# Mixing layer of a decoder block: T1 and T3 made in place as one tile, T4 and T2 made chunk by chunk in four idle tiles

## The chip, the cores and the metric

The kernel runs on one core of one Trainium2 chip. The metric is the device time of one execution in microseconds (us), as the median of the runs of a kernel; the profile and the trace are those of one further execution.

## What is computed

The reference is one layer of a decoder trunk over 1024 tokens of width 1024 in float32. The part around the change is the end of the token mixers and the start of the gated MLP:

```python
merged = sigmoid(g_da) * (y_da @ w_br_da) + sigmoid(g_sw) * (y_sw @ w_br_sw)
x  = x + merged @ w_mix_out
xn = rmsnorm(x, norm_ffn_w)
u  = xn @ w_up                          # 1024 -> 2 * 2816
c  = causal depthwise convolution of u, width 3, plus conv_b
x  = x + (silu(gate) * val) @ w_down    # gate, val: the halves of c
```

Before this stand the input projection and the two attentions, behind it a last rmsnorm. Every float32 matmul is done in three passes: both operands are split into a rounded high part and the rest (h and l), and the products h·h, h·l and l·h are added up. A split costs a cast on ScalarE and a subtraction on VectorE.

## The kernel before

Data lie transposed: 128 channels on the partitions, tokens along the free dimension, so x is eight chunks of 128 x 1024. The products with `w_up` are done with a seven-product scheme (Winograd's variant of Strassen) over 2 x 2 blocks. Chunk k (0 to 3) of the activations together with chunk k + 4 gives four blocks of 128 x 512: B11 and B12 are the token halves of chunk k, B21 and B22 those of chunk k + 4. From these come T1 = B12 - B11, T3 = B22 - B12, T2 = B22 - T1 and T4 = T2 - B21. The seven products are P1 = A11·B11, P2 = A12·B21, P5 = S1·T1, P7 = S3·T3, P3 = S4·B22, P6 = S2·T2 and P4 = A22·T4, where the A are blocks of a pair of weight tiles and the S are sums of them.

**The mixing layer, `mix` (L706 to L745).** Eight turns i, in the order of chunks 0, 4, 1, 5, 2, 6, 3, 7. Each has 48 matmuls with a tile of `w_mix` (L135 to L137, into `sc`), then VectorE adds x (L728), ScalarE stores x and scales it by the norm weight into a tile `xw` (L731), and ScalarE squares x (L740) while GpSimd adds the squares into `rstd` (L741). After every odd turn, `operands` (L747) makes the blocks of one k: it splits B11, B21, T1, T3 and B22 (each a cast L701 and a subtraction L702 of 128 x 512), with T1 and T3 first made on VectorE in small tiles (L758, L761), and T2 made unsplit on GpSimd (L764) into two tiles of the pool `cpl`, which the MLP later uses for its convolution. At i = 6 `sum_pair` (L78) makes the S of the first pair of weights on GpSimd (L87 to L90, into tiles `sf`).

**The up-projection, `hidden` (L777).** 22 turns j, one per pair of weight tiles. In turn 0 the first five products are done for k = 0 to 2; then the T2 are split (L800); then GpSimd rebuilds each B21 as the sum of its parts (L804), VectorE subtracts it from T2 to make T4 (L805), and T4 is split (L806); then the five products get k = 3, the squares are summed over the partitions by 16 small matmuls (L143), GpSimd makes the reciprocal root (L152), P6 and P4 follow, and eight transposes (L158) spread the root over the partitions, from where VectorE copies it (L818). In each later turn the order is P1, P2, P5, P6, P7, P3, P4, 84 matmuls (L773 to L775). `recombine` (L341) takes the seven sums from PSUM with one copy on ScalarE (L349) and seven operations on VectorE (L350 to L356); GpSimd scales the two results (L865); ScalarE begins the convolution (L868), VectorE adds its two other taps (L869, L870), ScalarE applies silu (L833) and VectorE multiplies (L834).

**The weights of a turn.** `sum_pair` loads g into a tile `raw` (L81) and v into a tile `rv` (L83) and makes two tiles of sums, `sa` (L87, L88: the S1 and S2) and `sb` (L89, L90: the S3 and S4), both from the pool `sfp`, which has two buffers, so each `sb` goes where the last `sb` was. `split_pair` (L92) casts (L100) and subtracts (L102): `wl<-raw` for A11 and A12, `sl<-sf` for the S, `wl<-rv` for A22. The sums of a turn are made some two turns ahead.

**What sets the order.** No order is written out by hand here. A planner walks the program with a cost for each instruction and gives each engine a fixed queue: an engine takes the first instruction in program order that is ready by these costs, and `high_priority` (L788) puts some ahead. On the chip each queue is worked off in that order. A tile of a pool can be written when the tile that had its buffer (or its place, where one pool was closed and another opened) has been read for the last time.

Of the kernel before, what the change touches and what calls it, by code (L numbers as in the profile page):

```python
# [47 lines left out]
class Trunk:  # L48
# [656 lines left out]
    def mix(self, mh, ml, mctx):  # L705


        nc, tc = self.nc, self.tc
        self.fctx = ExitStack()
        self.cpl = self.fctx.enter_context(tc.tile_pool(name="cpl", bufs=2, reuse_waits="tile"))  # L710
        self.xctx2 = ExitStack()
        xc = self.xctx2.enter_context(tc.tile_pool(name="xc", bufs=1, reuse_waits="tile"))
        self.B = {}
        xt = {(n, k, p): xc.tile([P, H2], F32R, name=f"{n}_{k}{p}") for n in ("B11", "B21", "T1", "T3", "B22") for k in range(4) for p in "hl"}
        self.sfp = self.xctx2.enter_context(tc.tile_pool(name="sfp", bufs=2, reuse_waits="tile"))
        self.t2 = [self.tl(self.cpl, [P, 2, H2], "c") for _ in range(2)]
        acc = self.rstd
        mact = lambda kc, hf: (mh[kc][:, hf * H2:(hf + 1) * H2], ml[kc][:, hf * H2:(hf + 1) * H2])
        with tc.tile_pool(name="xtp", bufs=2, side="right", reuse_waits="tile") as xtp:
            xw = {}  # L720
            for i, m in enumerate(self.mix_order):
                x2 = self.tl(xtp, [P, T], "x2")
                nc.sync.dma_start(x2, self.xT[m])
                w = self.next_w()
                ps = self.tl(self.psS, [P, T], "sc")
                self.mm3_both(ps, w, mact, late=(KC - 1,) if i == 0 else ())
                self.flush(0)
                nc.vector.tensor_tensor(x2, x2, ps, ALU.add)  # L728
                self.store(self.x2d[m], x2)
                xw[m] = self.tl(xtp, [P, T], "xw")  # L730
                nc.scalar.mul(xw[m], x2, self.vecs[:, C_NF + m:C_NF + m + 1])  # L731
                if i == 0:
                    nc.scalar.activation(acc, x2, AF.Square)
                if i == 6:
                    pair = self.sum_pair(self.wsrc.pop(0)[0], True)
                if i % 2:
                    self.operands(xt, xtp, xw, i // 2)
                for hf in range(2 if i else 0):
                    sq = self.tl(xtp, [P, H2], "t", bufs=3)
                    nc.scalar.activation(sq, x2[:, hf * H2:(hf + 1) * H2], AF.Square)  # L740
                    nc.gpsimd.tensor_tensor(acc[:, hf * H2:(hf + 1) * H2], acc[:, hf * H2:(hf + 1) * H2], sq, ALU.add)  # L741
            self.flush(0)
        mctx.close()
        self.pctx.close()
        return pair  # L745

    def operands(self, xt, xtp, xw, k):  # L747

        tt = self.nc.vector.tensor_tensor
        b11, b12, b21, b22 = (xw[kc][:, hf * H2:(hf + 1) * H2] for kc in (k, k + 4) for hf in range(2))  # L750

        def put(name, t):
            self.B[name, k] = self.split(xt[name, k, "h"], xt[name, k, "l"], t)
# [7 lines left out]
        tt(t3, b22, b12, ALU.subtract)  # L761
        put("T3", t3)
        put("B22", b22)
        self.nc.gpsimd.tensor_tensor(self.t2[k // 2][:, k % 2], b22, t1, ALU.subtract)  # L764
# [12 lines left out]
    def hidden(self, pair):  # L777
        nc, tc = self.nc, self.tc
        with ExitStack() as ctx:
            e = ctx.enter_context  # L780
            psF = e(tc.tile_pool(name="psF", bufs=8, space=PSUM, reuse_waits="tile"))
            self.psT = psF
            xc2 = e(tc.tile_pool(name="xc2", bufs=1, side="right", reuse_waits="tile"))
            self.uw = e(tc.tile_pool(name="uw", bufs=3, side="right", reuse_waits="tile"))
            tp = e(tc.tile_pool(name="tp", bufs=2, side="right", reuse_waits="tile"))
            prods = (("P1", "A11", "B11"), ("P2", "A12", "B21"), ("P5", "S1", "T1"), ("P7", "S3", "T3"),
                     ("P3", "S4", "B22"), ("P6", "S2", "T2"), ("P4", "A22", "T4"))
            with tc.high_priority(400):  # L788
                w0 = self.split_pair(*pair)
            for j in range(NF):  # L790
                w = self.next_w() if j else w0
                ps = {}
                if j == 0:

                    for name, a, b in prods[:5]:
                        ps[name] = self.tl(psF, [P, H2], "t")
                        self.product(ps[name], w[a], b, range(3), last=False)
                    for k in range(4):
                        t2 = self.t2[k // 2][:, k % 2]
                        self.B["T2", k] = self.split(*(xc2.tile([P, H2], F32R, name=f"T2_{k}{p}") for p in "hl"), t2)  # L800
                    for k in range(4):
                        t2 = self.t2[k // 2][:, k % 2]
                        b21 = self.tl(tp, [P, H2], ("s1", "u2", "u3", "u4")[k], bufs=1)
                        nc.gpsimd.tensor_tensor(b21, *(t.bitcast(F32) for t in self.B["B21", k]), ALU.add)  # L804
                        nc.vector.tensor_tensor(t2, t2, b21, ALU.subtract)  # L805
                        self.B["T4", k] = self.split(*(xc2.tile([P, H2], F32R, name=f"T4_{k}{p}") for p in "hl"), t2)  # L806
# [27 lines left out]
                nc.vector.tensor_tensor(c[0], c[0], c[1], ALU.mult)  # L834
# [214 lines left out]
```

## Time and profile before

| | |
|---|---|
| median of 3 runs | 1409.01 us (1406.46 to 1409.37) |
| profiled execution | 1411.19 us |
| span of its instructions | 1409.4 us |
| busy: PE, VectorE (DVE), ScalarE (ACT), GpSimd (POOL) | 97%, 69%, 44%, 33% |
| mean granted TensorE clock | 0.986 |
| mixing layer, first matmul to last | 616.5 to 704.8 us |
| up-projection, first matmul to last | 704.67 to 1144.3 us |

PE is the matmul engine, PEld its weight loads. A row of the timeline has the start and the length in us, the engine, the line, the operation, its output and inputs with the names of the program (numbers left out: B_0h can be B11, B21 or B22 of k = 0, and T_0h one of T1 to T4), a count, and in brackets the idle time of the engine ahead of it with what ended it. Rows with a count above 1 are several instructions merged, with their total time. A matmul row lasts 0.39 us because matmuls overlap; what one costs is the distance between two starts.

### The profile page before, as it was taken

How to read it: one execution, taken by the hardware profiler on the slowest of the kernel's cores; microseconds unless marked ns; L12 is line 12 of the kernel's file. 1: busy time of each engine (PE TensorE's matmuls, PEld its weight loads, DVE VectorE, ACT ScalarE, POOL GpSimd, SP SyncE). 2: the span in 40 equal slices, each digit the busy share in tenths (PEclk: the TensorE clock that was granted, in tenths of full speed). 3: DMA queues.
4: the chain of work that ended last, by engine and by line, in shares of the span. 5: the costliest groups of instructions: out<-in, count | busy, mean ns of one | idle time of the engine just before them, and what ended most of it. 6: DMA issues, size and time to landing. Idle time of an engine off the chain costs nothing.

```text
span 1409.4 us, 17228 instructions
## 1 busy us (share of the span) xinstructions
PE 1367.7 (97%) x6374; PEld 1121.9 (80%) x6374; DVE 972.8 (69%) x1408; ACT 624.6 (44%) x975; POOL 461.8 (33%) x326
## 2 busy tenths in 40 slices
PE   8899999999999999999999999999999999999997
PEld 6688888888888777878867778888888867888887
DVE  8966763887778855455499888888889896344332
ACT  8422322877756753334344333443333354233221
POOL 0446530000000033633476565555555441000001
PEclk9999999999999999999989999999999999999998
DMA  6244438755243263334411222222222258433432
GB/s 245 84 156 149 165 135 260 200 159 138 89 121 123 79 221 141 133 107 136 145 64 61 90 75 90 90 75 76 75 89 90 74 170 279 143 116 119 158 95 73
DMA packets 62196, 179.23 MB, mean 127 GB/s; under 512 B 6816, under 2 KB 13088, under 8 KB 62112
## 3 DMA queue, kind: packets, MB, share of 16 engines
q1 hardware_dynamic: 49648, 158.88, 35.2%
q10 hardware_dynamic: 12464, 19.25, 3.8%
q8 instruction: 50, 0.82, 0.2%
q14 instruction: 34, 0.28, 0.1%
HBM read 130.39 MB, written 47.71 MB: 126 GB/s over the span
## 4 chain that ended last, share of the span: by engine, by line
PE 56%; DVE 18%; issue 8%; POOL 7%; ACT 6%; DMA 4%; DVEq 0%; ACTq 0%; SPq 0%; POOLq 0%
PE d L900 16%; PE t L773 4%; PE t L774 4%; PE t L775 4%; POOL us L865 4%; PE g L135 3%; PE g L137 3%; PE g L136 3%; DVE wl L102 3%; PE sc L519 3%; DVE c L834 3%; DMA gr<-gd 2%; PE sc L137 2%; PE sc L135 2%; PE sc L136 2%
## 5 line engine op out<-in xcount | busy, mean ns | idle before, releaser
L900 PE MATMUL d<-h,wh 128*128 128x512 f32 (+1 forms) x680 | 202.7, 383 | 5.1 <-ACT h L701 2.3
L116 DVE TENSOR_TENSOR wl<-raw,wh 128x1024 fp32r<-128x1024 f32 (+1 forms) x79 | 98.6, 1248 | 144.3 <-ACT wh L114 140.0
L114 ACT CAST wh<-raw 128x1024 fp32r<-128x1024 f32 (+1 forms) x81 | 81.5, 1007 | 196.7 <-PE d L900 142.4
L900 PEld LDWEIGHTS d<-h,wh 128*128 128x128 f32 x680 | 126.2, 190 | 33.7 <-DVE h L702 5.2
L868 ACT ACTIVATE c<-us,vecs 128x1024 f32<-128x1024 f32 x44 | 54.8, 1248 | 168.6 <-POOL us L865 164.1
L900 PE MATMUL d<-h,wl 128*128 128x512 f32 (+1 forms) x340 | 123.9, 381 | 0.0
L100 ACT CAST sh<-sf 128x1024 fp32r<-128x1024 f32 x60 | 62.7, 1049 | 96.5 <-POOL sf L88 57.5
L865 POOL TENSOR_TENSOR us<-us,rstd 128x1024 f32<-128x1024 f32 x42 | 100.4, 2409 | 14.5 <-DVE us L355 10.2
L87 POOL TENSOR_TENSOR sf<-rv 128x512 f32<-128x512 f32 x29 | 40.4, 1393 | 191.7 <-DMA rv<-in_w_up 60.2
L869 DVE SCALAR_TENSOR_TENSOR c<-us,vecs,c 128x1024 f32<-128x1024 f32 x44 | 66.5, 1512 | 50.6 <-ACT c L868 50.6
L152 POOL TENSOR_TENSOR rs<-ms,mhalf 128x8 f32<-128x8 f32 (+2 forms) x9 | 13.7, 1518 | 245.0 <-DVE ms L150 236.3
L102 DVE TENSOR_TENSOR sl<-sf,sh 128x1024 fp32r<-128x1024 f32 x60 | 84.0, 1402 | 9.0 <-ACT sh L100 9.0
L137 PE MATMUL g<-xh,wl 128*128 128x512 f32 x224 | 89.4, 399 | 0.0
L136 PE MATMUL g<-xl,wh 128*128 128x512 f32 x224 | 89.2, 398 | 0.0
L135 PE MATMUL g<-xh,wh 128*128 128x512 f32 x224 | 88.9, 397 | 0.0
L677 POOL TENSOR_TENSOR gr<-gr,rstd 128x1024 f32<-128x1024 f32 x16 | 40.4, 2529 | 137.7 <-DMA gr<-gd 137.7
L900 PEld LDWEIGHTS d<-h,wl 128*128 128x128 f32 x340 | 65.0, 191 | 12.1
L870 DVE SCALAR_TENSOR_TENSOR c<-us,vecs,c 128x1024 f32<-128x1024 f32 x44 | 62.0, 1414 | 0.7
L523 DVE CUSTOM_DVE_ANT_0 L<-sc,bias 128x128 f32<-128x128 f32 (+7 forms) x64 | 47.7, 751 | 20.2 <-PE sc L519 15.9
L89 POOL TENSOR_TENSOR sf<-raw,rv 128x512 f32<-128x512 f32 x29 | 39.5, 1361 | 63.5 <-DVE sl L102 61.8
L88 POOL TENSOR_TENSOR sf<-sf,raw 128x512 f32<-128x512 f32 x30 | 57.6, 1919 | 1.6
L102 DVE TENSOR_TENSOR wl<-raw,wh 128x1024 fp32r<-128x1024 f32 (+1 forms) x31 | 56.9, 1835 | 0.0
(360 smaller groups left out, 3877.1 us busy)
## 6 DMA issues: line engine op xcount, KB each, us to landing
u<-qd SPq DMA_DIRECT2D x72, 256.0 KB, 7.2
raw<-in_w_down SPq DMA_DIRECT2D x32, 448.0 KB, 3.4
raw<-in_w_in SPq DMA_DIRECT2D x26, 512.0 KB, 4.0
raw<-in_w_up SPq DMA_DIRECT2D x23, 512.0 KB, 3.5
rv<-in_w_up SPq DMA_DIRECT2D x21, 512.0 KB, 3.5
hd<-c SPq DMA_DIRECT2D x20, 512.0 KB, 2.6
qd<-us SPq DMA_DIRECT2D x18, 512.0 KB, 2.6
hr<-hd SPq DMA_DIRECT2D x36, 256.0 KB, 4.5
```

Of the source, the lines that this page charges most:

```text
L88: tt(sa[:, 1], sa[:, 0], g[:, 0], ALU.subtract)
L100: nc.scalar.copy(hi, src)
L102: nc.vector.tensor_tensor(lo, src, hi.bitcast(F32), ALU.subtract)
L114: nc.scalar.copy(wh, raw)
L116: (eng or nc.vector).tensor_tensor(wl, raw, wh.bitcast(F32), ALU.subtract)
L135: nc.tensor.matmul(ps, wh[:, kc + o, :], ah, start=first and n == 0, stop=False)
L136: nc.tensor.matmul(ps, wh[:, kc + o, :], al, start=False, stop=False)
L137: nc.tensor.matmul(ps, wl[:, kc + o, :], ah, start=False, stop=last and n == len(kcs) - 1)
L865: (nc.vector if m % NF == NF - 1 else nc.gpsimd).tensor_tensor(us[:, 2:], us[:, 2:], self.rstd, ALU.mult)
L869: nc.vector.scalar_tensor_tensor(c, us[:, 1:T + 1], cw[1], c, ALU.mult, ALU.add)
L870: nc.vector.scalar_tensor_tensor(c, us[:, 0:T], cw[0], c, ALU.mult, ALU.add)
L900: nc.tensor.matmul(ps, v[:, k - k0, :], hs[hf, k][j][:, a:b], start=c == 0 and n == 0, stop=c == 2 and n == len(parts) - 1)
```

## The change

`mix` and `operands`:

- T1 and T3 of a k are made in place over chunk k's `xw` (T1 over B11, then T3 over B12), and the whole 128 x 1024 tile is split at once into tiles `T13`. The three other splits, B11, B21 and B22, stay.
- T2 and T4 are made on VectorE in the same place, for each k into one 128 x 1024 tile: two of `cpl`, one of `sfp`, and for k = 3 over chunk 7's own `xw`. T2 moves from GpSimd (L764) to VectorE.
- `sfp` gets a third buffer.
- The pool `xtp`, with the tiles x2, xw and t, lies on the left side of memory instead of the right and stays open into `hidden`.

`hidden`, turn 0: each of the four T42 tiles is split at once (four casts and four subtractions of 128 x 1024 in place of eight and eight of 128 x 512), and B21 is no longer rebuilt (L804) nor T4 made here (L805). Then `xtp` is closed, and the pool `tp` of the recombination is opened behind it.

```diff
-        xt = {... tile([P, H2]) for n in ("B11", "B21", "T1", "T3", "B22") for k in range(4) for p in "hl"}
-        self.sfp = ...tile_pool(name="sfp", bufs=2, reuse_waits="tile")
-        self.t2 = [self.tl(self.cpl, [P, 2, H2], "c") for _ in range(2)]
+        xt = {... tile([P, w]) for n, w in (("B11", H2), ("B21", H2), ("T13", T), ("B22", H2)) for k in range(4) for p in "hl"}
+        self.sfp = ...tile_pool(name="sfp", bufs=3, reuse_waits="tile")
+        self.t42 = [self.tl(self.cpl, [P, T], "c") for _ in range(2)] + [self.tl(self.sfp, [P, T], "sf")]
...
-        with tc.tile_pool(name="xtp", bufs=2, side="right", reuse_waits="tile") as xtp:
+        self.tctx = ExitStack()
+        xtp = self.tctx.enter_context(tc.tile_pool(name="xtp", bufs=2, reuse_waits="tile"))
...
     def operands(self, xt, xtp, xw, k):
         put("B11", b11)
         put("B21", b21)
-        t1 = self.tl(xtp, [P, H2], "t", bufs=3)
-        tt(t1, b12, b11, ALU.subtract)
-        put("T1", t1)
-        t3 = self.tl(xtp, [P, H2], "t", bufs=3)
-        tt(t3, b22, b12, ALU.subtract)
-        put("T3", t3)
         put("B22", b22)
-        self.nc.gpsimd.tensor_tensor(self.t2[k // 2][:, k % 2], b22, t1, ALU.subtract)
+        if k == 3:
+            self.t42.append(xw[k + 4])
+        t4, t2 = (self.t42[k][:, c] for c in (slice(0, H2), slice(H2, T)))
+        tt(b11, b12, b11, ALU.subtract)
+        tt(b12, b22, b12, ALU.subtract)
+        put("T13", xw[k])
+        tt(t2, b22, b11, ALU.subtract)
+        tt(t4, t2, b21, ALU.subtract)
...
     def hidden(self, pair):
-            tp = e(tc.tile_pool(name="tp", bufs=2, side="right", reuse_waits="tile"))
...
                     for k in range(4):
-                        t2 = self.t2[k // 2][:, k % 2]
-                        self.B["T2", k] = self.split(... T2_{k} ..., t2)
-                    for k in range(4):
-                        t2 = self.t2[k // 2][:, k % 2]
-                        b21 = self.tl(tp, [P, H2], ("s1", "u2", "u3", "u4")[k], bufs=1)
-                        nc.gpsimd.tensor_tensor(b21, *(t.bitcast(F32) for t in self.B["B21", k]), ALU.add)
-                        nc.vector.tensor_tensor(t2, t2, b21, ALU.subtract)
-                        self.B["T4", k] = self.split(... T4_{k} ..., t2)
+                        hi, lo = self.split(*(xc2.tile([P, T], F32R, name=f"T42_{k}{p}") for p in "hl"), self.t42[k])
+                        self.B["T4", k], self.B["T2", k] = ((hi[:, c], lo[:, c]) for c in (slice(0, H2), slice(H2, T)))
+                    self.tctx.close()
+                    tp = e(tc.tile_pool(name="tp", bufs=2, side="right", reuse_waits="tile"))
```

More of the change, by code (lines that the diff above doesn't have):

```diff
@@ L713, in mix @@
         self.B = {}
-        xt = {(n, k, p): xc.tile([P, H2], F32R, name=f"{n}_{k}{p}") for n in ("B11", "B21", "T1", "T3", "B22") for k in range(4) for p in "hl"}
-        self.sfp = self.xctx2.enter_context(tc.tile_pool(name="sfp", bufs=2, reuse_waits="tile"))
-        self.t2 = [self.tl(self.cpl, [P, 2, H2], "c") for _ in range(2)]
+        xt = {(n, k, p): xc.tile([P, w], F32R, name=f"{n}_{k}{p}") for n, w in (("B11", H2), ("B21", H2), ("T13", T), ("B22", H2)) for k in range(4) for p in "hl"}
@@ L717, in mix @@
+        self.sfp = self.xctx2.enter_context(tc.tile_pool(name="sfp", bufs=3, reuse_waits="tile"))
+        self.t42 = [self.tl(self.cpl, [P, T], "c") for _ in range(2)] + [self.tl(self.sfp, [P, T], "sf")]
         acc = self.rstd
         mact = lambda kc, hf: (mh[kc][:, hf * H2:(hf + 1) * H2], ml[kc][:, hf * H2:(hf + 1) * H2])
-        with tc.tile_pool(name="xtp", bufs=2, side="right", reuse_waits="tile") as xtp:
[L720 to L741, printed above, removed]
-            self.flush(0)
@@ new lines, in mix @@
+        self.tctx = ExitStack()
+        xtp = self.tctx.enter_context(tc.tile_pool(name="xtp", bufs=2, reuse_waits="tile"))
+        xw = {}
+        for i, m in enumerate(self.mix_order):
+            x2 = self.tl(xtp, [P, T], "x2")
+            nc.sync.dma_start(x2, self.xT[m])
+            w = self.next_w()
+            ps = self.tl(self.psS, [P, T], "sc")
+            self.mm3_both(ps, w, mact, late=(KC - 1,) if i == 0 else ())
+            self.flush(0)
+            nc.vector.tensor_tensor(x2, x2, ps, ALU.add)
+            self.store(self.x2d[m], x2)
+            xw[m] = self.tl(xtp, [P, T], "xw")
+            nc.scalar.mul(xw[m], x2, self.vecs[:, C_NF + m:C_NF + m + 1])
+            if i == 0:
+                nc.scalar.activation(acc, x2, AF.Square)
+            if i == 6:
+                pair = self.sum_pair(self.wsrc.pop(0)[0], True)
+            if i % 2:
+                self.operands(xt, xtp, xw, i // 2)
+            for hf in range(2 if i else 0):
+                sq = self.tl(xtp, [P, H2], "t", bufs=3)
+                nc.scalar.activation(sq, x2[:, hf * H2:(hf + 1) * H2], AF.Square)
+                nc.gpsimd.tensor_tensor(acc[:, hf * H2:(hf + 1) * H2], acc[:, hf * H2:(hf + 1) * H2], sq, ALU.add)
@@ L743, in mix @@
+        self.flush(0)
         mctx.close()
@@ L749, in operands @@
         tt = self.nc.vector.tensor_tensor
-        b11, b12, b21, b22 = (xw[kc][:, hf * H2:(hf + 1) * H2] for kc in (k, k + 4) for hf in range(2))
+        (b11, b12), (b21, b22) = ([xw[kc][:, hf * H2:(hf + 1) * H2] for hf in range(2)] for kc in (k, k + 4))
         def put(name, t):
-            self.B[name, k] = self.split(xt[name, k, "h"], xt[name, k, "l"], t)
+            hi, lo = self.split(xt[name, k, "h"], xt[name, k, "l"], t)
+            if name == "T13":
+                self.B["T1", k], self.B["T3", k] = ((hi[:, c], lo[:, c]) for c in (slice(0, H2), slice(H2, T)))
+            else:
+                self.B[name, k] = hi, lo
         put("B11", b11)
         put("B21", b21)
-        t1 = self.tl(xtp, [P, H2], "t", bufs=3)
-        tt(t1, b12, b11, ALU.subtract)
-        put("T1", t1)
-        t3 = self.tl(xtp, [P, H2], "t", bufs=3)
-        tt(t3, b22, b12, ALU.subtract)
-        put("T3", t3)
-        put("B22", b22)
-        self.nc.gpsimd.tensor_tensor(self.t2[k // 2][:, k % 2], b22, t1, ALU.subtract)
+        put("B22", b22)
+        if k == 3:
[6 more added lines that the diff above has]
+        tt(t4, t2, b21, ALU.subtract)
     def product(self, ps, a, b, ks=range(4), first=True, last=True):
@@ L798, in hidden @@
                     for k in range(4):
-                        t2 = self.t2[k // 2][:, k % 2]
-                        self.B["T2", k] = self.split(*(xc2.tile([P, H2], F32R, name=f"T2_{k}{p}") for p in "hl"), t2)
-                    for k in range(4):
-                        t2 = self.t2[k // 2][:, k % 2]
-                        b21 = self.tl(tp, [P, H2], ("s1", "u2", "u3", "u4")[k], bufs=1)
-                        nc.gpsimd.tensor_tensor(b21, *(t.bitcast(F32) for t in self.B["B21", k]), ALU.add)
-                        nc.vector.tensor_tensor(t2, t2, b21, ALU.subtract)
-                        self.B["T4", k] = self.split(*(xc2.tile([P, H2], F32R, name=f"T4_{k}{p}") for p in "hl"), t2)
+                        hi, lo = self.split(*(xc2.tile([P, T], F32R, name=f"T42_{k}{p}") for p in "hl"), self.t42[k])
+                        self.B["T4", k], self.B["T2", k] = ((hi[:, c], lo[:, c]) for c in (slice(0, H2), slice(H2, T)))
+                    self.tctx.close()
+                    tp = e(tc.tile_pool(name="tp", bufs=2, side="right", reuse_waits="tile"))
                     for name, a, b in prods[:5]:
```

## Prediction

> **What bounds the kernel now.** First the page: matmuls stand on PE nearly all the time.
>
> ```profile
> PE 1367.7 (97%) x6374; PEld 1121.9 (80%) x6374; DVE 972.8 (69%) x1408; ACT 624.6 (44%) x975; POOL 461.8 (33%) x326
> ```
>
> So time can only be lost or won where PE stands still or waits. I read two places: the seam between mixing layer and up-projection, which the change rewrites, and the 21 equal turns behind it, where a buffer is added. The seam on PE, by the timeline; then its clock, by the windows (the third number from the end is the granted clock):
>
> ```profile
> 716.23 0.39 PE L773 MATMUL t<-T_3h,sh 128*128 128x512 f32 x1
> 718.66 1.05 PE L143 MATMUL t<-ones,rstd 128*128 128x1 f32 x8 [0.23 <-POOL rstd L741]
> 720.33 1.05 PE L143 MATMUL t<-ones,rstd 128*128 128x1 f32 x8 [0.62 <-POOL rstd L741]
> 728.22 0.50 PE L774 MATMUL t<-T_0l,wh 128*128 128x512 f32 x1 [2.36 <-DVE T_0l L702]
> 732.91 1.97 PE L158 MATMUL t<-ident,rs 128*128 128x128 f32 x8 [0.28 <-POOL rs L152]
> 734.53 0.78 PE L773 MATMUL t<-B_0h,wh 128*128 128x512 f32 x1
> ```
> ```profile
> 724.00:726.00 2.00, 1.86 (x5) 0.90 (x3) 2.00 (x3) 0.70 (x2) 2.00 (x2) 0.50 0.00 0
> 734.00:736.00 2.00, 2.00 (x9) 1.71 (x8) 2.00 (x2) 0.00 (x0) 1.92 (x2) 0.50 0.63 238
> ```
>
> PE waits 0.23 and 0.62 us for GpSimd's sum of squares, 2.36 us for the first low part of T4, 0.28 us for the reciprocal root, and runs at half clock (0.50) for a time. Why T4 is late shows on VectorE and GpSimd:
>
> ```profile
> 708.88 1.78 DVE L761 TENSOR_TENSOR t<-xw,xw 128x512 f32<-128x512 f32 x1
> 715.69 1.77 DVE L702 TENSOR_TENSOR T_0l<-c,T_0h 128x512 fp32r<-128x512 f32 x1
> 722.43 1.76 DVE L805 TENSOR_TENSOR c<-c,s 128x512 f32<-128x512 f32 x1
> 724.12 3.44 DVE L805 TENSOR_TENSOR c<-c,u 128x512 f32<-128x512 f32 x2
> 727.49 0.68 DVE L702 TENSOR_TENSOR T_0l<-c,T_0h 128x512 fp32r<-128x512 f32 x1
> 731.27 1.22 DVE L102 TENSOR_TENSOR wl<-raw,wh 128x1024 fp32r<-128x1024 f32 x1
> 733.55 0.68 DVE L351 TENSOR_TENSOR u<-t,s 128x512 f32<-128x512 f32 x1
> 738.38 1.22 DVE L102 TENSOR_TENSOR sl<-sf,sh 128x1024 fp32r<-128x1024 f32 x1 [1.67 <-ACT sh L100]
> 742.51 0.68 DVE L355 TENSOR_TENSOR us<-t,u 128x512 f32<-128x512 f32 x1
> ```
> ```profile
> 707.90 2.20 POOL L87 TENSOR_TENSOR sf<-rv 128x512 f32<-128x512 f32 x1 [7.86 <-DVE sl L102]
> 710.07 1.74 POOL L764 TENSOR_TENSOR c<-xw,t 128x512 f32<-128x512 f32 x1
> 716.88 3.40 POOL L741 TENSOR_TENSOR rstd<-rstd,t 128x512 f32<-128x512 f32 x2
> 720.24 1.72 POOL L804 TENSOR_TENSOR s<-B_0h,B_0l 128x512 f32<-128x512 f32 x1
> 730.73 2.13 POOL L152 TENSOR_TENSOR rs<-ms,mhalf 128x8 f32<-128x8 f32 x1 [3.64 <-DVE ms L150]
> ```
>
> The reader is to see 1.7 for 128 x 512 operations of VectorE that take 0.68 at 727.49, just while GpSimd works, at 1.7 an operation too: the two engines take turns. That tie costs 1.1 us per VectorE operation, some ten times.
>
> Now a late turn, on PE, VectorE and GpSimd, and two rows of the waits from 736 to 1144 us (in total, times, longest):
>
> ```profile
> 873.52 0.39 PE L773 MATMUL t<-B_0h,wh 128*128 128x512 f32 x1
> 874.07 0.50 PE L775 MATMUL t<-B_0h,wl 128*128 128x512 f32 x1
> 892.83 0.39 PE L773 MATMUL t<-B_0h,wh 128*128 128x512 f32 x1
> 1133.41 0.39 PE L773 MATMUL t<-T_0h,sh 128*128 128x512 f32 x1
> 1136.13 0.39 PE L773 MATMUL t<-T_0h,sh 128*128 128x512 f32 x1
> ```
> ```profile
> 870.07 1.72 DVE L834 TENSOR_TENSOR c<-c,c 128x1024 f32<-128x1024 f32 x1
> 871.70 2.31 DVE L102 TENSOR_TENSOR wl<-raw,wh 128x1024 fp32r<-128x1024 f32 x1
> 873.93 0.68 DVE L351 TENSOR_TENSOR u<-t,s 128x512 f32<-128x512 f32 x1
> 874.53 1.21 DVE L102 TENSOR_TENSOR sl<-sf,sh 128x1024 fp32r<-128x1024 f32 x1
> 877.77 0.69 DVE L355 TENSOR_TENSOR us<-t,u 128x512 f32<-128x512 f32 x1
> 882.77 1.73 DVE L869 SCALAR_TENSOR_TENSOR c<-us,vecs,c 128x1024 f32<-128x1024 f32 x1 [2.58 <-ACT c L868]
> ```
> ```profile
> 870.78 2.15 POOL L88 TENSOR_TENSOR sf<-sf,raw 128x512 f32<-128x512 f32 x1
> 875.82 1.30 POOL L89 TENSOR_TENSOR sf<-raw,rv 128x512 f32<-128x512 f32 x1 [2.90 <-DVE sl L102]
> 878.54 4.88 POOL L865 TENSOR_TENSOR us<-us,rstd 128x1024 f32<-128x1024 f32 x2
> ```
> ```profile
> POOL sf L89 <- DVE sl L102: 57.1, 19, 5.7
> PEld t L775 <- DVE wl L102: 11.0, 18, 2.1
> ```
>
> Twelve matmuls take 1136.13 - 1133.41 = 2.72 us, so 84 take 19.04. The turn takes 892.83 - 873.52 = 19.31. PE loses the difference at its third matmul, which waits for `wl` of VectorE (874.07; 18 such waits of weight loads). And VectorE waits for PE nowhere in that list: its own ring is L355, GpSimd's scaling (878.54), ScalarE, L869 (idle 2.58 us until then), on to `wl`, `sl` and the next L355. **In the turns this ring, not PE, sets the pace, by about 0.3 us a turn.** What lengthens the ring costs up to 21 times; what the seam wins counts as far as it starts the ring earlier. The ring's start is the L355 at 742.51.
>
> **The change, part by part.** Sums against the profiled execution, 1411.19 us (span 1409.4 and 1.8 around it), 2.2 above the median of 1409.01; I carry differences over to the median.
>
> *Mixing layer, turns 0 to 6: nothing.* VectorE gains two subtractions of 0.68 per k, GpSimd loses one; by the groups of lines VectorE idles before each x + sc there, 35.0 us in eight, ended by PE alone:
>
> ```profile
> L728 DVE TENSOR_TENSOR x<-x,sc 128x1024 f32<-128x1024 f32 x8 | 9.8, 1222 | 35.0 <-PE sc L137 35.0
> ```
> No DMA is moved past a queue. T1 in place waits for B11's split, and T2 and T4 of k = 3 for those of B22 and B21; the next xw waits for T13's split and T4, two turns back.
>
> *Seam, VectorE.* Now, from 708.88: T3's subtraction, three splits of k = 3, four of T2, four subtractions and four splits for T4, the last just before 731.27. New: T3's subtraction, B21 and B22 (0.6 each from start to start), T13, T2, T4, and four T42 of 128 x 1024 at 1.14 (starts from 731.27 on less their overlap of 0.08). Without GpSimd that is 5 x 0.6 + 5 x 1.14 = 8.7 us. GpSimd still has L87 (at 707.90) to L90 and two L741, six operations that take turns with it; each adds 1.1 us: 15.3, so it ends at 724.2. GpSimd ends earlier as well: without the 1.74 of L764 the last L741 ends not at 720.28 but near 719.
>
> *Seam, PE.* T1's split of k = 3 used to be done a turn before; now it comes with T13, which ends between 716.3 and 718.0, depending on whether T2 is queued ahead of it. PE wants it at 716.23 plus 0.2: a wait of 0 to 1.6 us, behind which stand the last products of k = 3 and the small matmuls. As these wait for L741 until 719 anyway, little of it counts. P6 can then start at 720.5 to 722; late next is its last low part, at 724.2. P4 ends near 727.6. The root's chain (L152, 2.13) starts behind T42 at 725 instead of 730.73 and is done by then, so the eight transposes end near 728.6, against 734.53: 5.9 us earlier on PE. Half clock again on eight of the 24 matmuls (0.23 more for each, a twelfth of the 2.72 above) would leave 4.2.
>
> The Trainium skill, "TensorE: Matmul & The Clock Gate", Part 1, says that the array falls to half rate after at least one idle window of about 3.4 us. Here it stands at 0.50 at 724, with no idle stretch over 0.62 us in the seam before that, so the trace does not bear the rule out as it stands. By the rule the new seam would stay at full clock and 5.9 would be the lower end.
>
> *Seam, the ring's start.* From L351 at 733.55 to L355 it now takes 9.0 us, of which 1.67 is the wait at 738.38 for S of turn 2: GpSimd made it late, since its buffer was that of the S of turn 1. With the third buffer that wait goes. New: 724.2, then L350 (0.6, as L351) and the small input of L152, 0.8 together, two splits for turn 1 at 1.14, then L351 at 727.3, and 9.0 - 1.7 = 7.3 to the L355: 734.6 to 735.5 with a turn taken with GpSimd's S. **Won: 7 us** (bounds 4.2, PE's at half clock, and 8.5, with another operation or two of GpSimd out of the way).
>
> The pool `tp` now lies over `xtp`, so its first writes (L349, L350) wait for T42 of k = 3 to be read, at 724.2; both come behind it anyway. The two `c` tiles are first wanted by L868, behind the L355 of turn 0. In the down-projection h tiles come to lie over T13 in place of T1; its last reader is P7 instead of P5, still two products before the end. Nothing.
>
> *The third buffer of `sfp`, in the turns.* This decides. At 875.82 L89 starts after an idle 2.90 us because its `sb` goes where the last `sb` was, and that is read by the `sl` of 874.53. With three buffers, used in rotation, it goes where an `sa` was that was read a turn before: the 19 waits of the row go, and L89 follows L88 directly. Its place moves from beside L352 to L355, which read PSUM and aren't slowed (877.77: 0.69), to beside `wl` and `sl`. L88 ends at 872.93, `wl` has the turn until 874.01, then L89: L88 needed 872.93 - 871.79 = 1.14 after L834 let go, so L89 ends at 875.15. `sl`, due at 874.53, waits and ends 1.08 after that (as `wl` after L88), at 876.23 instead of 875.74: **0.49 us a turn, on the ring**. L90 then runs beside PSUM readers. Over 19 turns 9.3 us; in the first two L89 and L90 meet three or four such operations (about 1 us more), so 10.2. From below: 0, if `sl` goes first or the queue is planned otherwise. Below nothing I exclude: at its present place L89 makes nobody wait (L865 starts at L355's end). From above: 1.3 us, all of L89's length (875.82) before `sl`, 19 times, 25. I take 0.49, from the rows of L88 and `wl`, the same pair of engines one operation earlier.
>
> The Trainium skill, "GPSIMD Engine Reference", 1. Specifications, says that GpSimd shares its SBUF interfaces with VectorE, with contention for VectorE instructions with two SBUF inputs. `sl` is one, L352 to L355 are not, so by it L89 hurts at its new place and not at its old; the rows of `wl` (2.31) and L355 (0.69) agree. It gives no price.
>
> Sum: -7.0 + 10.2 = **+3.2**, 1409.0 + 3.2 = **1412.2 us**.
>
> **The rivals.**
>
> *A, forecast:* seam won, more lost in the turns: 1412.2, from 1409 to 1416. For it: the constant 2.58 us of idle before L869, VectorE's ring closed without PE. 45%.
>
> *B, faster:* the third buffer costs nothing, because the planner, which sees L89 ready earlier, queues the sums or `sl` elsewhere, beside the PSUM readers where nobody waits; then the won 7 stay: 1402, from 1400 to 1405. It decides below 0.37 us a turn (7.0 / 19): above it the kernel isn't faster. 30%.
>
> *C, dearer:* `sl` waits L89's whole 1.3 us in half of the turns: 9.5 x 1.3 + 9.5 x 0.49 = 17, 1409 - 7 + 17 = 1419. For it: 2.31 for `wl` now, a whole operation's wait. 15%.
>
> *D, no change:* T13's late split and a new half-clock stretch eat the seam's gain to 4 or 5, and the turns cost 4 or 5: 1409. 10%.
>
> **How the numbers follow.** Likeliest is A: 1412.2. About 0.2%, 2.8 us, is what a measurement of this kernel can tell from no change. A lies above 1411.8 in some 26 of its 45, within in 18, faster in 1; B gives 29 faster, 1 within; C 15 slower; D 9 within, 1 slower. Together 30 faster, 28 within, 42 slower. The range 1400 to 1419 takes in B and half of C; A's own range is 1409 to 1416.
>
> **What would show it.** Right: no L804, T4's wait gone at P4, P1 of turn 1 near 728 to 729, L355 of turn 0 near 735; behind it L89 starting within 1.5 us of L88's end, `sl` at 1.7, and turns of 19.7 to 19.9. Wrong: turns still at 19.3 (B), at 20.3 or more (C), or P1 of turn 1 after 731 (D). What I can't see is the planner's new queue order; that would upset most of this.

## The result, and the profile after

| | before | after |
|---|---|---|
| median | 1409.19 us (1406.46 to 1409.82, 4 runs) | 1417.21 us (1415.41 to 1419.70, 4 runs) |
| profiled execution, span | 1411.19, 1409.4 us | 1415.97, 1414.2 us |
| up-projection: first matmul of turn 0, first of the down-projection | 704.67, 1144.29 us | 701.17, 1148.63 us |

The changed kernel takes 8.0 us more; the ratio is 1.0062, interval 1.0040 to 1.0084. The lines below are numbered as in the changed kernel: most stand 2 or 3 further down than before (L865 is L868, L834 is L837, L773 is L781).

One difference between the two profiled executions has to be taken out first. The third number from the end of a row of the windows is the granted clock; before is the first fence, after the second:

```profile
520.00:540.00 20.00, 16.24 (x58) 12.41 (x57) 9.48 (x7) 8.68 (x10) 6.80 (x2) 0.83 0.63 226
```
```profile
520.00:540.00 20.00, 15.30 (x64) 11.38 (x62) 11.67 (x10) 8.37 (x9) 6.24 (x2) 1.00 0.62 229
```

TensorE was slowed for a while at 520 to 540 us before, and not after (20 us at 0.83 instead of 1.00 are 3.4 us short). That is ahead of all code that the change touches, where the mixing layer's first matmul already stands at 613.1 us after and at 616.5 before; so the up-projection's earlier start, 3.5 us, is not the change's doing. So stretches are counted from here on from turn 0's first matmul (704.67 and 701.17). So counted, the down-projection begins after 439.62 us before and after 447.46 us after: 7.8 us later, nearly all of the 8.0 us between the medians.

The seam after, on PE, VectorE and GpSimd by the timeline:

```profile
701.17 0.39 PE L781 MATMUL t<-B_0h,wh 128*128 128x512 f32 x1
714.84 1.93 PE L143 MATMUL t<-ones,rstd 128*128 128x1 f32 x16
...
717.40 0.50 PE L782 MATMUL t<-T_0l,sh 128*128 128x512 f32 x1 [0.30 <-DVE T_0l L702]
...
721.84 0.39 PE L781 MATMUL t<-T_0h,wh 128*128 128x512 f32 x1
...
730.20 1.97 PE L158 MATMUL t<-ident,rs 128*128 128x128 f32 x8 [5.45 <-POOL us L867]
731.82 0.78 PE L781 MATMUL t<-B_0h,wh 128*128 128x512 f32 x1
```
```profile
710.50 2.32 DVE L702 TENSOR_TENSOR T_3l<-xw,T_3h 128x1024 fp32r<-128x1024 f32 x1
...
719.54 1.21 DVE L702 TENSOR_TENSOR T_3l<-xw,T_3h 128x1024 fp32r<-128x1024 f32 x1
720.67 2.30 DVE L102 TENSOR_TENSOR sl<-sf,sh 128x1024 fp32r<-128x1024 f32 x1
...
731.35 0.69 DVE L821 COPY rstd<-t 128x512 f32<-128x512 f32 x1 [0.81 <-PE t L158]
...
734.00 0.69 DVE L355 TENSOR_TENSOR us<-t,u 128x512 f32<-128x512 f32 x1
```
```profile
719.69 2.20 POOL L87 TENSOR_TENSOR sf<-rv 128x512 f32<-128x512 f32 x1 [4.03 <-DVE T_2l L702]
...
726.29 2.25 POOL L90 TENSOR_TENSOR sf<-raw,sf 128x512 f32<-128x512 f32 x1
728.50 1.64 POOL L152 TENSOR_TENSOR rs<-ms,mhalf 128x8 f32<-128x8 f32 x1
```

The column sums no longer wait (714.84). T4's wait of 2.36 us at P4 is gone (P4 starts at 721.84); since T2 and T4 are now split together, PE waits for that split earlier, at P6, and for only 0.30 us (717.40). T42 is split by 720.75 (719.54 + 1.21). But the eight transposes stand idle for 5.45 us: in GpSimd's queue the root (L152, 728.50) stands behind the four sums of turn 2 (719.69 to 728.5). So P1 of turn 1 comes 731.82 - 701.17 = 30.65 us after turn 0's start, where it was 734.53 - 704.67 = 29.86. The ring's first L355, though, comes at 32.83 in place of 37.84, 5.0 us earlier.

A late turn after, VectorE and GpSimd:

```profile
908.47 1.72 DVE L837 TENSOR_TENSOR c<-c,c 128x1024 f32<-128x1024 f32 x1
910.12 2.30 DVE L102 TENSOR_TENSOR wl<-raw,wh 128x1024 fp32r<-128x1024 f32 x1
912.35 0.68 DVE L351 TENSOR_TENSOR u<-t,s 128x512 f32<-128x512 f32 x1
912.95 1.71 DVE L102 TENSOR_TENSOR sl<-sf,sh 128x1024 fp32r<-128x1024 f32 x1
...
916.68 0.69 DVE L355 TENSOR_TENSOR us<-t,u 128x512 f32<-128x512 f32 x1
```
```profile
907.79 1.32 POOL L87 TENSOR_TENSOR sf<-rv 128x512 f32<-128x512 f32 x1 [5.23 <-DMA rv<-in_w_up]
...
909.11 2.23 POOL L89 TENSOR_TENSOR sf<-raw,rv 128x512 f32<-128x512 f32 x1
911.30 2.28 POOL L88 TENSOR_TENSOR sf<-sf,raw 128x512 f32<-128x512 f32 x1
913.65 2.16 POOL L90 TENSOR_TENSOR sf<-raw,sf 128x512 f32<-128x512 f32 x1
```

`sl` took 1.21 us before and GpSimd stood idle for 2.90 us ahead of L89. Now the four sums run without a gap, in the order L87, L89, L88, L90, and stand beside L837, `wl`, `sl` in turn: `sl` starts at 912.95, gets its turn only when L88 lets go at 913.58, and ends 1.08 us after that. The mean of all splits `sl` from 800 to 1100 us, by the groups of lines (busy, mean in ns), before and after:

```profile
L102 DVE TENSOR_TENSOR sl<-sf,sh 128x1024 fp32r<-128x1024 f32 x31 | 37.6, 1212 | 0.0
```
```profile
L102 DVE TENSOR_TENSOR sl<-sf,sh 128x1024 fp32r<-128x1024 f32 x30 | 43.9, 1462 | 0.0
```

0.25 us more in the mean, two `sl` in a turn: 0.50 us a turn. The ring's own rate, from L355 of turn 2 to that of turn 19, agrees. Before and after:

```profile
780.78 0.69 DVE L355 TENSOR_TENSOR us<-t,u 128x512 f32<-128x512 f32 x1
...
1110.23 0.69 DVE L355 TENSOR_TENSOR us<-t,u 128x512 f32<-128x512 f32 x1
```
```profile
777.82 0.69 DVE L355 TENSOR_TENSOR us<-t,u 128x512 f32<-128x512 f32 x1
...
1115.07 0.69 DVE L355 TENSOR_TENSOR us<-t,u 128x512 f32<-128x512 f32 x1
```

329.45 us before and 337.25 after in 17 turns: 19.38 and 19.84. In the first two turns of the ring the loss is larger still, 38.27 us before (742.51 to 780.78) and 43.82 after (734.00 to 777.82). So -5.0 at the ring's start, +5.5 in its first two turns and +7.8 in the other seventeen, +8.3 in all; the 7.8 above are at the down-projection, which follows the last turn 0.5 us sooner than before.

### The profile page after: what moved, and what is told of

The parts are those of the page before. It is cut to its first block, busy times and chain, and to the rows that moved or that the text cites. A ratio compares the mean times of both kernels' runs of the same rounds, so it can differ in the third digit from the quotient of the medians.

```text
span 1414.2 us, 17204 instructions
## 1 busy us (share of the span) xinstructions
PE 1364.1 (96%) x6374; PEld 1119.4 (79%) x6374; DVE 985.7 (70%) x1404; ACT 624.1 (44%) x967; POOL 494.3 (35%) x318
## 4 chain that ended last, share of the span: by engine, by line
PE 53%; DVE 17%; issue 9%; POOL 8%; ACT 6%; DMA 5%; DVEq 0%; ACTq 0%; SPq 0%; POOLq 0%
PE d L903 16%; POOL us L868 4%; PE t L781 4%; PE t L783 4%; PE t L782 4%; DVE wl L102 3%; PE g L135 3%; PE g L136 3%; PE g L137 3%; DVE c L837 3%; PE sc L519 3%; DMA gr<-gd 2%; PE sc L137 2%; DVE c L873 2%; PE sc L136 2%
## 5 line engine op out<-in xcount | busy, mean ns | idle before, releaser
L116 DVE TENSOR_TENSOR wl<-raw,wh 128x1024 fp32r<-128x1024 f32 (+1 forms) x79 | 98.7, 1249 | 145.7 <-ACT wh L114 145.4
L868 POOL TENSOR_TENSOR us<-us,rstd 128x1024 f32<-128x1024 f32 x42 | 100.3, 2408 | 53.1 <-DVE us L355 49.1
L87 POOL TENSOR_TENSOR sf<-rv 128x512 f32<-128x512 f32 x29 | 41.6, 1435 | 193.2 <-DMA rv<-in_w_up 81.5
L102 DVE TENSOR_TENSOR sl<-sf,sh 128x1024 fp32r<-128x1024 f32 x60 | 93.9, 1566 | 7.4 <-ACT sh L100 7.4
L152 POOL TENSOR_TENSOR rs<-ms,mhalf 128x8 f32<-128x8 f32 (+2 forms) x9 | 13.2, 1464 | 238.0 <-DVE ms L150 229.3
L873 DVE SCALAR_TENSOR_TENSOR c<-us,vecs,c 128x1024 f32<-128x1024 f32 x44 | 63.1, 1438 | 0.7
L90 POOL TENSOR_TENSOR sf<-raw,sf 128x512 f32<-128x512 f32 x30 | 61.7, 2058 | 1.6
L89 POOL TENSOR_TENSOR sf<-raw,rv 128x512 f32<-128x512 f32 x29 | 58.3, 2009 | 6.4 <-DVE sl L102 4.6
L88 POOL TENSOR_TENSOR sf<-sf,raw 128x512 f32<-128x512 f32 x30 | 60.2, 2006 | 0.8
```

The costliest lines, as they stand in the source:

```text
L90: tt(sb[:, 1], g[:, 1], sa[:, 1], ALU.subtract)
L102: nc.vector.tensor_tensor(lo, src, hi.bitcast(F32), ALU.subtract)
L116: (eng or nc.vector).tensor_tensor(wl, raw, wh.bitcast(F32), ALU.subtract)
L868: (nc.vector if m % NF == NF - 1 else nc.gpsimd).tensor_tensor(us[:, 2:], us[:, 2:], self.rstd, ALU.mult)
L873: nc.vector.scalar_tensor_tensor(c, us[:, 0:T], cw[0], c, ALU.mult, ALU.add)
```

## The experiments

The theory: the third buffer takes away L89's wait, GpSimd's sums then run beside VectorE's operations with two SBUF inputs, and this makes both the turns and the start of the ring dearer; the new seam by itself is a gain. Rival 1: the wide tiles made in place are what slows the turns. Rival 2: it is the planner's new order of the sums, not the lost wait. Rival 3: the seam's gain was lost to the root's place behind four sums.

All times by the ring, in one table; start is L355 of turn 0 after turn 0's first matmul, the ratio is to the kernel before, run beside each. "Turns 0 to 2" runs from the L355 of turn 0 to that of turn 2, "17 turns" from there to turn 19; a turn is a 17th of it, and the sum is that of the three stretches.

| kernel | median us | ratio (interval) | start | turns 0 to 2 | 17 turns | a turn | sum |
|---|---|---|---|---|---|---|---|
| before | 1408 to 1411 | 1 | 37.84 | 38.27 | 329.45 | 19.38 | 405.56 |
| after | 1417.21 | 1.0062 (1.0040 to 1.0084) | 32.83 | 43.82 | 337.25 | 19.84 | 413.90 |
| e1: two buffers | 1404.59 | 0.9962 (0.9949 to 0.9976) | 30.91 | 39.48 | 329.17 | 19.36 | 399.56 |
| e2: before, three buffers | 1422.09 | 1.0086 (1.0072 to 1.0099) | 38.56 | 41.81 | 338.09 | 19.89 | 418.46 |
| e3: three buffers, `sb` waits | 1403.57 | 0.9954 (0.9940 to 0.9968) | 30.78 | 39.47 | 327.67 | 19.27 | 397.92 |
| e4: after, root first | 1420.02 | 1.0073 (1.0060 to 1.0085) | 33.51 | 43.74 | 336.90 | 19.82 | 414.15 |
| e5: e1, root first | 1407.05 | 0.9978 (0.9968 to 0.9989) | 32.33 | 39.50 | 329.37 | 19.37 | 401.20 |
| e6: after, `sb` behind L88 | 1420.15 | 1.0074 (1.0060 to 1.0087) | 33.95 | 42.20 | 339.56 | 19.97 | 415.71 |
| e7: after, L90 a copy | 1415.76 | 1.0042 (1.0028 to 1.0056) | 31.50 | 42.45 | 336.82 | 19.81 | 410.77 |
| e8: e1, small T1 and T3 | 1403.65 | 0.9956 (0.9942 to 0.9970) | 29.93 | 39.48 | 328.99 | 19.35 | 398.40 |
| e9: e3 and e8 | 1401.84 | 0.9954 (0.9938 to 0.9971) | 30.75 | 39.48 | 328.01 | 19.29 | 398.24 |

**e1, two buffers again.** The memory stays as in the changed kernel:

```diff
-self.sfp = ...tc.tile_pool(name="sfp", bufs=3, reuse_waits="tile"))
+self.sfp = ...tc.tile_pool(name="sfp", bufs=2, reuse_waits="tile"))
+t4p = ...tc.tile_pool(name="t4p", bufs=1, reuse_waits="tile"))
-self.t42 = [...] + [self.tl(self.sfp, [P, T], "sf")]
+self.t42 = [...] + [self.tl(t4p, [P, T], "t4")]
```

> The changed kernel, with two `sfp` buffers again; the third T4/T2 tile gets a pool of its own, in the same memory. So L89 has to wait for the `sl` split of the sum before it, as in the kernel before. Theory (the third buffer made the turns longer, by a GpSimd sum that now runs beside a VectorE split): steady turns fall from 19.83 to about 19.35 us, 20 turns by 9 us; the root stands in GpSimd's queue behind two sums of turn 2 in place of four, so turn 1's P1 comes 1 to 4 us earlier; in all 1404 to 1409 us. Rival (the wide in-place tiles of the new mixing layer slow the hidden layer, whatever the buffers): turns stay at 19.8 and the time at 1416 to 1418 us.

Measured: 1404.59 us, 0.38% faster than the kernel before. The waits and the seam of its VectorE:

```profile
POOL sf L89 <- DVE sl L102: 60.0, 19, 5.7
```
```profile
722.05 1.21 DVE L102 TENSOR_TENSOR sl<-sf,sh 128x1024 fp32r<-128x1024 f32 x1
...
723.86 1.91 DVE L102 TENSOR_TENSOR wl<-raw,wh 128x1024 fp32r<-128x1024 f32 x1
...
742.74 3.50 DVE L874 SCALAR_TENSOR_TENSOR c<-us,vecs,c 128x1024 f32<-128x1024 f32 x2
746.16 1.21 DVE L102 TENSOR_TENSOR wl<-raw,wh 128x1024 fp32r<-128x1024 f32 x1
...
766.18 1.21 DVE L102 TENSOR_TENSOR wl<-raw,wh 128x1024 fp32r<-128x1024 f32 x1
767.32 1.21 DVE L838 TENSOR_TENSOR c<-c,c 128x1024 f32<-128x1024 f32 x1
```

The 19 waits of L89 are back and the turn is at 19.36. The first two turns of the ring fall from 43.82 to 39.48, and four operations account for it. The changed kernel has:

```profile
723.57 1.64 DVE L102 TENSOR_TENSOR wl<-raw,wh 128x1024 fp32r<-128x1024 f32 x1
...
743.34 4.54 DVE L873 SCALAR_TENSOR_TENSOR c<-us,vecs,c 128x1024 f32<-128x1024 f32 x2
747.80 2.31 DVE L102 TENSOR_TENSOR wl<-raw,wh 128x1024 fp32r<-128x1024 f32 x1
...
768.92 2.31 DVE L102 TENSOR_TENSOR wl<-raw,wh 128x1024 fp32r<-128x1024 f32 x1
771.15 2.31 DVE L837 TENSOR_TENSOR c<-c,c 128x1024 f32<-128x1024 f32 x1
```

L873 4.54 against 3.50 (L874 in e1), `wl` 2.31 against 1.21, again 2.31 against 1.21, and L837 2.31 against 1.21 (L838 in e1): 1.04 + 3 x 1.10 = 4.34, all of the difference. At the ring's start `sl` takes 1.21 (722.05) in place of 2.30 (720.67), which is 1.1 of the 1.9 us won there. Another 0.97 are VectorE's two waits for the spread root in the changed kernel (0.81 at 731.35, and 0.16), of which e1 has none; a `wl` that is 0.27 longer in e1 (723.86) takes some back. P1 of turn 1 comes 2.0 us earlier than in the changed kernel. Rival 1 has fallen: the wide tiles are all still there.

**e2, the kernel before with three buffers.**

```diff
-self.sfp = ...tc.tile_pool(name="sfp", bufs=2, reuse_waits="tile"))
+self.sfp = ...tc.tile_pool(name="sfp", bufs=3, reuse_waits="tile"))
```

> The kernel before, with nothing changed but `sfp` from two buffers to three. Theory (the third buffer is the cause of the longer turns): `sl` at 1.7 us in place of 1.2, turns of 19.8 us in place of 19.36, 7 to 9 us more than the kernel before, 1416 to 1418 us. Rival (the wide tiles are the cause): turns unchanged, 1409 us.

Measured: 1422.09 us, 11.6 above the kernel before (1410.52 beside it), more than was expected. Its `sl`:

```profile
L102 DVE TENSOR_TENSOR sl<-sf,sh 128x1024 fp32r<-128x1024 f32 x30 | 43.8, 1461 | 0.0
```

This one edit does by itself what the whole change did to the turns (1461 ns; by the table 338.09 us in 17 turns, +8.6), adds 3.5 us in the first two, and 0.7 at the start. The expectation had missed the first two turns. e1 and e2 together show the two parts with their signs: the new seam alone is worth -6 us (medians and ring), the third buffer alone +12 (11.6 by the medians, 12.9 by the ring). The two do not quite add up: by the ring -6.0 + 12.9 is 6.9, where the whole change costs 8.3. Together with the new seam the third buffer costs 14.3 (after against e1).

**e3, three buffers, but L89 waits.** `sa` rotates through two, `sb` has one of its own:

```diff
-sb = self.tl(self.sfp, [P, 2, 4, P], "sf")
+sb = self.tl(self.sfb, [P, 2, 4, P], "sb") if self.sfb else self.tl(self.sfp, [P, 2, 4, P], "sf")
...
-self.sfp = ...tc.tile_pool(name="sfp", bufs=3, reuse_waits="tile"))
+self.sfp = ...tc.tile_pool(name="sfp", bufs=2, reuse_waits="tile"))
+self.sfb = ...tc.tile_pool(name="sfb", bufs=1, reuse_waits="tile"))
```

> The changed kernel with its three buffers in another order: `sa` rotates through two, and `sb` has one of its own, so that L89 must wait until `sl` of the `sb` before has been read. Memory, tiles and number of buffers are as in the changed kernel; only the wait is back. Theory (it is the lost wait that lets the sums run beside VectorE's `wl` and `sl`): `sl` back at 1.2 us, steady turns of 19.36 us, ring's first two turns at 39.5 us in place of 43.8, 1404 to 1406 us, as with two buffers. Rival (a third buffer as such, or where the tiles lie, makes the turn longer): 19.8 us a turn, 1416 to 1418 us.

Measured: 1403.57 us. Waits and splits (L90 here is the L89 of the changed kernel):

```profile
POOL sb L90 <- DVE sl L103: 60.0, 19, 5.7
```
```profile
L103 DVE TENSOR_TENSOR sl<-sb,sh 128x1024 fp32r<-128x1024 f32 x16 | 19.3, 1209 | 0.0
```

As many bytes of sum tiles as in the changed kernel, and no loss. So it is not a third buffer as such. With the wait the sums also stand in their old order again, as in e1, so the wait and the order are not yet told apart; e6 does that. Why a turn is 19.27 and not 19.36 here stays open.

**e6, the old order without the wait.** One small copy ties `sb` to `sa`:

```diff
+if not first:
+    nc.gpsimd.tensor_copy(sb[:, 0, 0, :8], sa[:, 1, 0, :8])
 tt(sb[:, 0], g[:, 0], v[:, 0], ALU.subtract)
```

> The changed kernel with one small GpSimd copy (8 columns of `sa` into `sb`) that puts both sums of `sb` behind L88 in GpSimd's queue, as they stood in the kernel before, but with no wait for `sl`. The prediction's term (sums of `sb` that follow L88 directly run beside `sl`, whatever stands between L87 and L88): steady turns of 19.8 to 19.9 us, 1416 to 1419 us. Rival (the planner's new order L87, L89, L88, L90 makes the turn longer, not the lost wait): 19.36 us a turn, 1405 to 1409 us.

Measured: 1420.15 us and 19.97 us a turn, with the mean of all `sl` from 800 to 1100 us, and one of them (lines lie up to 2 further down here):

```profile
L104 DVE TENSOR_TENSOR sl<-sf,sh 128x1024 fp32r<-128x1024 f32 x31 | 47.3, 1526 | 0.0
```
```profile
912.29 2.31 DVE L104 TENSOR_TENSOR wl<-raw,wh 128x1024 fp32r<-128x1024 f32 x1
...
915.12 1.86 DVE L104 TENSOR_TENSOR sl<-sf,sh 128x1024 fp32r<-128x1024 f32 x1
```

`sl` takes 0.31 us more than before in the mean, twice a turn, where the turn is 0.59 longer. Both sums of `sb` stand behind L88 again, though the second (L92) now ahead of the first (L91), and `sl` at 915.12 is held by L92, which ends at 915.90. Part of that is the copy's own price, as L92 can start only behind it, at 914.61. Without the copy L92 would have its turn when `wl` ends at 914.52 and need 1.14, as L88 did in the prediction, and `sl` would end 1.08 after that, at 916.74: by this estimate 1.62 in place of 1.21. So rival 2, in which the planner's order and not the lost wait makes the turn longer, has fallen: behind L88 and without a wait the sums cost about as much.

**e4 and e5, the root first.** In the changed kernel and in e1, a small copy of the root into turn 2's first sum tile holds turn 2's sums behind the root:

```diff
-rs = self.rstd_cols(ssq, 8, D)
+rs = self.root = self.rstd_cols(ssq, 8, D)
...
+self.nsum += self.root is not None
+if self.nsum == 2:
+    nc.gpsimd.tensor_copy(sa[:, 0, 0, :8], self.root)
 tt(sa[:, 0], v[:, 0], v[:, 1], ALU.add)
```

> The changed kernel with its three buffers, and one small GpSimd copy (8 columns of the root into turn 2's first sum tile, which L87 then overwrites), so that turn 2's sums stand behind the root in GpSimd's queue. Theory (the seam's gain was lost to those four sums): the root starts within 1 us of the end of `ms`, some 4.5 us earlier, TensorE's wait of 5.45 us at the spread falls below 1 us, P1 of turn 1 comes 4 to 5 us earlier, steady turns stay at 19.8: 1412 to 1413.5 us. Rival (turn 2's sums are now late by the same 4.5 us and turns 1 to 3 give it back): the spread is early, but the start of turn 4 is where it was: 1416 to 1418 us.

Measured for e4: 1420.02 us; ratio 1.0073, beside 1.0062 for the changed kernel, so no gain. PE and VectorE (lines lie 5 further down here: L163 is L158, L107 is L102):

```profile
728.13 1.09 PE L163 MATMUL t<-ident,rs 128*128 128x128 f32 x8 [0.74 <-POOL rs L157]
...
753.65 0.80 PE L788 MATMUL t<-B_0h,wl 128*128 128x512 f32 x1 [4.91 <-DVE wl L107]
```
```profile
733.29 1.34 DVE L107 TENSOR_TENSOR sl<-sf,sh 128x1024 fp32r<-128x1024 f32 x1 [4.18 <-ACT sh L105]
```

The transposes wait 0.74 us in place of 5.45, and P1 of turn 1 comes 24.94 us after turn 0's start, 5.7 earlier. But already at the third matmul of turn 2 PE stands for 4.91 us at `wl` (753.65). In VectorE's queue `sl` of turn 2 stands ahead of what turn 0 still needs, and it now waits 4.18 us (733.29), for the cast of a sum that comes later. The ring starts at 33.51, no earlier than after's 32.83. So an earlier spread by this edit wins nothing, and rival 3, the theory in e4's text, isn't borne out. As the edit puts in a wait of its own (4.18 us), the run alone doesn't show what the early spread would be worth. That can be read from the changed kernel, where VectorE waits for the spread for 0.81 and 0.16 us: of PE's idle 5.45 us about 1 was on the ring.

> Both edits in one: two `sfp` buffers, and turn 2's sums behind the root. If the two causes are separate they add: 1402 to 1405 us, faster than the kernel before by 4 to 7 us, with turns of 19.35 us. If turn 2's sums then come late (they wait for the root and for a free buffer), turns 1 to 3 give 3 to 5 us back: 1406 to 1409 us. If the wide tiles were the cause of the turns, 1412 us or more.

Measured for e5: 1407.05 us, 2.5 more than e1 beside it (1.6 by the ring), which fits the second expectation. The start of the ring is 1.4 later than e1's, for the same reason: `sl` of turn 2 waits 3.07 us for its cast.

**e7, one of the sums a copy with one input.** S4's subtraction is left out:

```diff
-tt(sb[:, 1], g[:, 1], sa[:, 1], ALU.subtract)
+nc.gpsimd.tensor_copy(sb[:, 1], sa[:, 1])
```

> The changed kernel with L90 made a copy with one input (`sb[:, 1]` becomes a copy of `sa[:, 1]`: the subtraction from `g` is left out, so S4 is not the operand that the layer needs). Theory A (a GpSimd instruction takes turns with VectorE only where it reads two tiles): `sl`, beside which L90 runs, falls from 1.71 to 1.21 us, steady turns of 19.36 us, first two turns of the ring still 43 to 44 us (L88 and L89 stay): 1409 us. Theory B (any GpSimd instruction on SBUF takes turns): `sl` stays near 1.7 us if the copy lasts as long as the subtraction, turns of 19.8 us, 1416 to 1418 us.

Measured: 1415.76 us, 19.81 us a turn. `sl` kept its 1.71 us, as theory B had it, but the rows show that the run couldn't tell the two apart by `sl`:

```profile
911.20 2.27 POOL L88 TENSOR_TENSOR sf<-sf,raw 128x512 f32<-128x512 f32 x1
913.54 1.49 POOL L90 COPY sf<-sf 128x512 f32<-128x512 f32 x1
```
```profile
912.85 1.71 DVE L102 TENSOR_TENSOR sl<-sf,sh 128x1024 fp32r<-128x1024 f32 x1
```

`sl` is held by L88, which ends at 913.47, and not by L90, which starts only then. The 3.1 us by which its ring is shorter than the changed kernel's lie mostly at the start and in the first two turns (1.3 and 1.4). What bears on the question came with e4 and e6, in which a copy of 128 x 8 stands in a free place (first row) and beside `wl` (second). The third row, of e6 too, is a MEMSET, which reads no tile:

```profile
728.14 0.19 POOL L90 COPY sf<-rs 128x8 f32<-128x8 f32 x1
```
```profile
913.57 1.07 POOL L90 COPY sf<-sf 128x8 f32<-128x8 f32 x1
```
```profile
911.22 0.10 POOL L869 MEMSET us<- 128x2 f32 x1
```

0.19 us alone, 1.07 behind a `wl` that lasts until VectorE's next instruction starts at 914.52. A GpSimd instruction with one input takes its turn with VectorE too, and theory A falls. Theory B goes too far with "any": the MEMSET is done at 911.32, while VectorE's L839 (910.53 to 912.36), which had let L87 pass until 911.28, works on.

**e8 and e9, the wide T13 taken back.** e8 is e1 with T1 and T3 split apart:

```diff
 tt(b11, b12, b11, ALU.subtract)
+put("T1", b11)
 tt(b12, b22, b12, ALU.subtract)
-put("T13", xw[k])
+put("T3", b12)
```

> The two-buffer version of the changed kernel, with T1 and T3 split again as two tiles of 512 columns, T1 ahead of T3 (in place of one tile of 1024). If the one wide tile costs nothing (the prediction's term for T13: no wait at P5): 1404 to 1406 us, as the two-buffer version. If T13, whose low half ends 712.8 us in the changed kernel's trace, holds the products of slice 3 or the ring's start, the small tiles give 0.5 to 1 us: 1403.5 us. If the two extra instructions on VectorE and ScalarE push the T4/T2 splits back, 1 to 2 us more: 1406 to 1407 us.

> The two best edits in one: T1 and T3 as two tiles of 512 columns, and three buffers of which `sb` has one alone, so that its sums wait for `sl`. By the ring: a start 30 us after turn 0's first matmul, 39.5 us for the first two turns, 17 turns of 19.27 to 19.36 us: 1402 to 1404 us, 6 to 8 us less than the kernel before. If the small tiles win nothing on top of the other edit, 1403.5 us; if GpSimd's order at the seam changes against them, 1405 us or more.

Measured: 1403.65 us for e8 and 1401.84 for e9; the ratios, 0.9956 and 0.9954, can't be told from e1's 0.9962 and e3's 0.9954. The ring starts 1.0 us earlier in e8 than in e1, but in e9 no earlier than in e3; one profile of each doesn't settle whether T13 costs anything. e9 has the lowest median of all, 0.46% under the kernel before (0.29 to 0.62%); e1, e3 and e8 are as good within their intervals.

## Why the prediction was right, and where it was not

- **Way and range:** forecast 1412.2 (1400 to 1419), measured 1417.21. Slower, by the mechanism of A; the size lies just above A's own range (1409 to 1416).
- **What bounds it: right.** The ring sets the pace, not PE. In e4 PE began turn 1 5.7 us earlier, the ring started no earlier, and no time was won.
- **Turns: right.** 0.49 us a turn was worked out, 0.46 measured (e1 against after: 0.48; e2 against before: 0.51), `sl` at 1.71. The planner put L89 ahead of L88, which I had not foreseen, so that L88 and not L89 holds `sl`; the price is nearly the same, as e6 shows for the other order. The sign "L89 starting within 1.5 us of L88's end" was so not met as written. Of the rivals, B's "queues the sums elsewhere" came true in its condition and not in its effect.
- **First two turns: the term that was mis-sized.** "Three or four such operations (about 1 us more)": four it was, but each costs 1.0 to 1.1 us, as the prediction's own row of `wl` (2.31 against 1.22) had it, so 4.3 (after against e1), not 1. The other 1.2 of the 5.5 is still there in e1 (39.48 against 38.27). With 4.3 in place of 1 the forecast would have been 1415.5, and with 5 in place of 7 at the ring's start 1417.5. That this comes so close to 1417.21 is partly luck: the missing 1.2 is made up by the turns, where 9.3 us for 19 stand against 7.8 measured in 17.
- **Ring's start: right for the new seam, too high for the whole change.** VectorE's stretch from T3's subtraction to the last T42 was forecast at 15.3 us and took 15.4 (705.39 to 720.75). 7 us was predicted for the ring, and e1 has 37.84 - 30.91 = 6.9. That sum is better than its steps: in e1 a further `sl` stands ahead of L351, which comes 2.8 us later than forecast, and from there to L355 it takes 5.5 us in place of 7.3. The changed kernel has 5.0. The third buffer takes the rest here too, as the prediction had not counted: turn 2's sums find a free buffer as soon as T42_2 is read (719.69) and run beside `sl`, and the spread comes 1 us late for VectorE.
- **PE at the seam: wrong, with about 1 us of effect on the ring.** "The root's chain is done by then" failed: the root stood behind four sums of turn 2, and P1 of turn 1 came 0.8 us later, not 5.9 earlier. By the mark set for it (P1 after 731) that pointed to D. D's first reason, T13's late split, did not occur: it ends at 712.82 (710.50 + 2.32), and PE's column sums start at 714.84, behind T13's products, with no wait. Its second, a stretch at half clock, is in the trace (0.53 at 718 to 720 us, 0.50 at 730 to 734), but before had as much (0.50 at 724 to 726 and 730 to 736). The lower bound of 4.2 is a small slip: 5.9 - 8 x 0.23 is 4.1. L355 of turn 0, at 734.0, met the forecast "near 735" only because the up-projection began 3.5 us early; counted from its start it was some 2.5 us late.
- **The Trainium skill's two rules.** "GPSIMD Engine Reference", 1. Specifications, has contention with VectorE instructions that have two SBUF inputs. The traces agree: `sl`, `wl`, L837 and L873 lengthen beside GpSimd's sums, and L350 to L356 stay at 0.68 or 0.69. The Trainium skill's "TensorE: Matmul & The Clock Gate", Part 1, was put to no run of its own, and by it the prediction had the new seam at full clock. The traces agree with it in part: behind the idle 5.45 us of the changed kernel the clock is at 0.50 (730 to 734), and in e4, where the same wait is 0.74, it stays at 1.00 (724 to 738). But the 0.53 at 718 to 720 us stands behind 16 small matmuls, with no idle stretch over 0.30 us in the seam before it.

## What to carry to other kernels

A wait in a trace can be what keeps two engines off each other. Before a buffer is added to remove it, look at what the freed instruction will run beside, and price every neighbour at the length that the rows show under contention, first of all in the irregular turns at the start. And count a gain only at the engine whose ring sets the pace: 5.7 us won on PE in e4 left the ring's start where it was and were worth nothing; 6.9 us at the ring's start in e1 were worth 6.

## What the runs showed of the hardware

- GpSimd and VectorE took turns by whole instructions, where VectorE's has two inputs in SBUF and GpSimd's reads a tile, however small: a copy of 128 x 8 with one input took 0.19 us in a free place (e4) and 1.07 us beside `wl` (e6). A MEMSET of 128 x 2, which reads none, took 0.10 us beside VectorE's L839 (e6).
- Each of VectorE's two-input operations on 128 x 1024 that met a GpSimd sum of 128 x 512 lost 0.4 to 1.1 us, as it came in midway or had to let a whole sum pass (`wl` 1.21 to 1.64 at 723.57 in the changed kernel, `sl` 1.21 to 1.71, `wl` and L837 1.21 to 2.31).
